# Fewer, wider products in a two-layer decoder: high and low part of x in one matmul, and the first layer's down projection with tokens on partitions

## The chip, the cores and the metric

The kernel runs on one core of a Trainium2 chip. The metric is the device time of one execution in microseconds (us); each kernel is run several times and the median counts. The core has five engines with a queue of instructions each: TensorE (PE in the profile, its weight loads PEld), VectorE (DVE), ScalarE (ACT), GpSimd (POOL) and SyncE (SP), which here issues nearly all DMAs.

## The reference, cut to what matters

Two layers work on 256 tokens of width 1024. In each, a normalized x is projected to queries, keys, values and gates, 24 heads of three kinds of attention follow, and their outputs go through three branch projections, gates and one output projection, which is added to x. Then comes an MLP with a squared ReLU, added to x as well:

```python
merged = gates[:, :, 0] * y_a + gates[:, :, 1] * y_b + gates[:, :, 2] * y_c
x = x + merged @ w_o                                  # output projection
h = rmsnorm(x, norm_mlp)
return x + jnp.square(jax.nn.relu(h @ w_up)) @ w_down # up and down projection
```

w_o is 1024x1024, w_up 1024x4096, w_down 4096x1024, all float32. One normalization follows the second layer.

## The kernel before, in words

All large products run in a rounded float32 form on TensorE, and exactness is kept by splitting: each operand is a high part (rounded) plus a low part (the rest), and a product is three matmuls, low weight by high x, high weight by high x, and high weight by low x. x lies transposed in SBUF, `xres[P, 8, 256]`: 128 channels on partitions, 8 channel tiles (index d or k), 256 tokens.

Weights arrive in 140 pieces of 128x1024 (512 KB) for each layer, in the order in which they are used; `split_one` makes a high part `wh` on ScalarE (L115) and a low part `wl` on VectorE (L116). Four raw buffers and six split buffers turn over. Splits are issued ahead of the work around them (`tc.high_priority`, three pieces ahead).

`proj` (L190 to L197) computes one 128-channel output tile for 256 tokens: for each of 8 k three matmuls of 256 columns, L195 with `lo`, L196 with `hi`, L197 with `hi` and the low part of x. It serves the query, key and gate projections, the branch outputs, the output projection and the up projection. High and low part of x lie in one tile `hl[P, 2, 8, 256]`.

The output projection loops over eight d. Each takes a PSUM bank (`mm_bank` and `t_bank` in turn, two of each), and VectorE adds the bank to `xres` (L511), ScalarE writes the next high part of x times the norm's weight (L155), VectorE its low part (L156), ScalarE squares (L165) and GpSimd adds the squares up (L166). `rms_cols` (L172) turns the sum into one factor for each token, `bcast` (L185) spreads it over partitions; in the first layer its square is `R2`.

The MLP runs over 16 pairs of up tiles. `up_pair` puts both tiles of a pair into the two halves of one bank; ScalarE takes the ReLU from there (L544) and squares (L546), VectorE writes high and low part (L549, L550). The two down products of a pair come one pair later. In the first layer `down` has channels on partitions: for each j and each of 8 d three matmuls of 256 columns (L561 to L563), 768 in all, into `acc2` (two double banks). In the last layer `down_nat` has tokens on partitions: `u` is the stationary operand, 512 weight columns move, in four groups (t, h) of three matmuls for each j (L587 to L589), 384 in all; for its sum x is transposed there (L576) and copied (L577).

At the end of a layer the last TAIL = 4 steps j are done group by group, so that results come out one after another. In the first layer, each d then gets a multiplication by R2 (L648), an addition to xres (L649) and the norm's split; the second layer's values follow (`v_chunk`, L245 to L247: 512 columns, k outermost, so that they can begin with k = 0 before the last d is done). Each engine takes its instructions in the order of a schedule that was laid out when the program was built; within it, ready work of later steps can stand ahead of steps that wait.

Of the kernel before, what the change touches and what calls it, by code (L numbers as in the profile page):

```python
# [41 lines left out]
TAIL = 4  # L42
SKEW = 2
UNIT_RATE = {"v": 2, "qk": 1, "g": 2}
# [14 lines left out]
def trunk(ctx: ExitStack, tc: tile.TileContext, w, x, norms, gfin, consts, out):  # L59
# [18 lines left out]
    def mm_bank():  # L78
        return PS("mm", [P, 512], 2)
# [4 lines left out]
    def t_bank():  # L84
        return PS("t", [P, 512], 2)
# [63 lines left out]
    def hilo_slot():  # L149
        return T("hl", [P, 2, KT, S], 2, F32R)  # L150

    def norm_split(hl, nrm, d):

        g = cst["norms"][:, nrm, d:d + 1]
        act.activation(hl[:, 0, d], xres[:, d], AF.Copy, scale=g)  # L155
        dve.scalar_tensor_tensor(hl[:, 1, d], xres[:, d], g, hl[:, 0, d].bitcast(F32),  # L156
                                 op0=ALU.mult, op1=ALU.subtract)
# [30 lines left out]
    def proj(dst, n, hl, nk=KT, first=True, last=True, koff=0, woff=0):  # L188

        hi, lo = split(n)  # L190
        for k in range(nk):
            c = (woff + k) * P
            a = (first and k == 0)
            z = (last and k == nk - 1)
            pe.matmul(dst, lo[:, c:c + P], hl[:, 0, koff + k], start=a, stop=False, skip_group_check=True)  # L195
            pe.matmul(dst, hi[:, c:c + P], hl[:, 0, koff + k], start=False, stop=False, skip_group_check=True)  # L196
            pe.matmul(dst, hi[:, c:c + P], hl[:, 1, koff + k], start=False, stop=z, skip_group_check=True)  # L197

# [11 lines left out]
    for layer in range(DEPTH):  # L210
# [9 lines left out]
        def normalized():  # L220

            for d in range(KT):
                t = T("sq", [P, S], 3)
                g = cst["norms"][:, 2 * layer, d:d + 1]
                dve.scalar_tensor_tensor(t, xres[:, d], g, R, op0=ALU.mult, op1=ALU.mult)
                act.activation(xh[:, 0, d], t, AF.Copy)
                dve.tensor_tensor(xh[:, 1, d], t, xh[:, 0, d].bitcast(F32), op=ALU.subtract)  # L227

# [3 lines left out]
        def v_chunk(c, n):  # L232
# [5 lines left out]
            for q in range(4):  # L238
                hi, lo = split(n + q)
                for kk in range(2):  # L240
                    k = 2 * q + kk
                    wsl = slice(kk * 512, kk * 512 + 512)
                    for t in range(2):
                        tsl = slice(t * P, t * P + P)
                        pe.matmul(pv[t], xs[:, 0, k, tsl], lo[:, wsl], start=k == 0, stop=False)  # L245
                        pe.matmul(pv[t], xs[:, 0, k, tsl], hi[:, wsl], start=False, stop=False)
                        pe.matmul(pv[t], xs[:, 1, k, tsl], hi[:, wsl], start=False, stop=k == KT - 1)  # L247
            V[c] = T("V", [P, 2, 8, 2, DH], 3, F32R)
# [47 lines left out]
        def o_split(oF, kt):  # L296
            last_exp[0] = act.activation(oT[:, 0, kt], oF, AF.Copy)
            dve.tensor_tensor(oT[:, 1, kt], oF, oT[:, 0, kt].bitcast(F32), op=ALU.subtract)

# [190 lines left out]
        for d in range(KT):  # L490
# [10 lines left out]
            dve.tensor_tensor(m3[:, 0], m3[:, 0], m3[:, 2], op=ALU.add)  # L501
            act.activation(mg[:, 0, d], m3[:, 0], AF.Copy)
            dve.tensor_tensor(mg[:, 1, d], m3[:, 0], mg[:, 0, d].bitcast(F32), op=ALU.subtract)

# [15 lines left out]
        n = base + 76  # L520
        acc2 = [s_bank(), s_bank()]

        def down_dst(d):
            return acc2[d % 2][:, d // 2 % 2, d // 4 * S:(d // 4 + 1) * S]

# [13 lines left out]
        def up_pair(i):  # L539
            p = mm_bank()  # L540
            proj(p[:, 0:S], npc["u", 2 * i], hl)
            proj(p[:, S:2 * S], npc["u", 2 * i + 1], hl)
            s1 = T("wk", [P, 512], WK)
            act.activation(s1, p, AF.Relu)  # L544
            u = T("wk", [P, 512], WK)
            act.activation(u, s1, AF.Square)  # L546
            uh = T("ga", [P, 2, S], KT, F32R)
            ul = T("ga", [P, 2, S], KT, F32R)
            dve.tensor_copy(uh.rearrange("p a b -> p (a b)"), u)  # L549
            dve.tensor_tensor(ul.rearrange("p a b -> p (a b)"), u, uh.rearrange("p a b -> p (a b)").bitcast(F32), op=ALU.subtract)  # L550
            us[i] = (uh, ul)


        def down(j, d):
            hi, lo = split(npc["d", j])
            uh, ul = us[j // 2]
            a = j == 0 and d < 4
            z = j == 2 * npairs - 1
            dst = down_dst(d)
            c = slice(d * P, d * P + P)  # L560
            pe.matmul(dst, lo[:, c], uh[:, j % 2], start=a, stop=False, skip_group_check=True)  # L561
            pe.matmul(dst, hi[:, c], uh[:, j % 2], start=False, stop=False, skip_group_check=True)  # L562
            pe.matmul(dst, hi[:, c], ul[:, j % 2], start=False, stop=z, skip_group_check=True)  # L563

        last = layer == DEPTH - 1
        if last:
# [5 lines left out]
            for t in range(2):  # L572
                for h in range(2):
# [3 lines left out]
                    dve.tensor_copy(xn[t][h], tb)  # L577
            r2 = T("rc", [P, 2], 8)
            dve.tensor_tensor(r2, rcol, rcol, op=ALU.mult)

# [55 lines left out]
        hl = hilo_slot()  # L636
        for d in range(KT):
            if d == 0:
                for e in range(SKEW):
                    for j in range(body, 2 * npairs - 2):  # L640
                        down(j, e)
            if d + SKEW < KT:
# [106 lines left out]
```

## Time and profile before

| | |
|---|---|
| median of 3 runs | 893.87 us (893.34 to 893.88) |
| the profiled execution's own time | 893.46 us |
| its span, first to last instruction | 891.4 us |
| TensorE busy | 878.8 us, 99% |
| VectorE busy | 602.4 us, 68% |
| ScalarE busy | 491.7 us, 55% |
| GpSimd busy | 52.4 us, 6% |
| DMA | 151.47 MB, mean 170 GB/s |
| mean granted TensorE clock | 0.998 of full speed (2.4 GHz) |

A matmul's duration in the profile overlaps the next one's; how fast TensorE goes is read from the distance between two starts, not from the durations. The shares are means over the whole span; the stages differ.

### The profile page before, as it was taken

The page shows a single profiled execution, that of the slowest core. Times are in us where ns is not written, and L with a number is a line of the kernel's source. Part 1 is how long each engine was busy: PE and PEld are TensorE (multiplying, and loading weights), DVE is VectorE, ACT ScalarE, POOL GpSimd, SP SyncE. Part 2 cuts the span into 40 slices and gives each one's busy share as a digit, 9 for nine tenths or more (in the row PEclk, how much of TensorE's full clock was granted, in tenths as well). Part 3 has the DMA queues.
Part 4 walks back from the last instruction along what each step waited for, and adds up shares of the span by engine and source line. Part 5 has one row for each costly group of instructions (what it writes and reads, how often), then busy time and mean ns, then how long its engine had stood idle before and what let it go on. Part 6 is the DMA issues. An engine that isn't in the chain of part 4 may idle for free.

```text
span 891.4 us, 16382 instructions
## 1 busy us (share of the span) xinstructions
PE 878.8 (99%) x6672; PEld 837.8 (94%) x6672; DVE 602.4 (68%) x899; ACT 491.7 (55%) x724; POOL 52.4 (6%) x72
## 2 busy tenths in 40 slices
PE   8999999999999999999999999999999999999996
PEld 6899999999999999999988999999999999999995
DVE  7887787774985455555588878777667865555554
ACT  5655566668465444444466555666573654444442
POOL 6000000000020000000020100000000400000000
PEclk9999999999999999999999999999999999999999
DMA  8764444544656656555556544444555666666641
GB/s 302 232 197 144 140 129 138 158 147 131 199 167 192 193 183 189 182 177 185 165 176 203 167 148 136 141 125 139 164 165 168 194 197 192 186 186 189 187 137 47
DMA packets 43562, 151.47 MB, mean 170 GB/s; under 512 B 4960, under 2 KB 6368, under 8 KB 43488
## 3 DMA queue, kind: packets, MB, share of 16 engines
q1 hardware_dynamic: 43056, 149.90, 54.6%
q8 instruction: 52, 0.85, 0.4%
q10 hardware_dynamic: 432, 0.54, 0.2%
q14 instruction: 22, 0.18, 0.1%
HBM read 149.37 MB, written 1.05 MB: 169 GB/s over the span
## 4 chain that ended last, share of the span: by engine, by line
PE 94%; DVE 3%; issue 1%; DMA 1%; ACT 0%; SPq 0%; POOLq 0%; DVEq 0%; ACTq 0%
PE mm L195 18%; PE mm L197 18%; PE mm L196 18%; PE s L561 3%; PE s L563 3%; PE s L562 3%; PE s L587 3%; PE s L588 3%; PE s L589 3%; PE s L280 2%; PE s L195 2%; PE s L197 2%; PE s L196 2%; PE s L245 2%; DVE wl L116 2%; PE s L247 2%
## 5 line engine op out<-in xcount | busy, mean ns | idle before, releaser
L116 DVE TENSOR_TENSOR wl<-raw,wh 128x1024 fp32r<-128x1024 f32 (+1 forms) x282 | 345.5, 1228 | 228.2 <-ACT wh L115 227.4
L115 ACT ACTIVATE wh<-raw 128x1024 fp32r<-128x1024 f32 (+1 forms) x282 | 295.2, 1051 | 296.4 <-PE mm L197 160.8
L195 PE MATMUL mm<-hl,wl 128*128 128x256 f32 x1344 | 383.2, 285 | 1.4 <-DVE xres L511 1.4
L196 PE MATMUL mm<-hl,wh 128*128 128x256 f32 x1344 | 381.5, 284 | 0.0
L197 PE MATMUL mm<-hl,wh 128*128 128x256 f32 x1344 | 380.1, 284 | 0.0
L195 PEld LDWEIGHTS mm<-hl,wl 128*128 128x128 f32 x1344 | 257.1, 191 | 5.8 <-DVE xres L511 1.8
L196 PEld LDWEIGHTS mm<-hl,wh 128*128 128x128 f32 x1344 | 257.1, 191 | 0.9
L197 PEld LDWEIGHTS mm<-hl,wh 128*128 128x128 f32 x1344 | 256.5, 191 | 0.7 <-DVE hl L227 0.2
L561 PE MATMUL s<-ga,wl 128*128 128x256 f32 x256 | 72.5, 284 | 0.0
L562 PE MATMUL s<-ga,wh 128*128 128x256 f32 x256 | 72.3, 283 | 0.0
L563 PE MATMUL s<-ga,wh 128*128 128x256 f32 x256 | 72.2, 283 | 0.0
L587 PE MATMUL s<-wl,ga 128*128 128x512 f32 x128 | 50.1, 391 | 0.0
L588 PE MATMUL s<-wh,ga 128*128 128x512 f32 x128 | 50.0, 391 | 0.0
L561 PEld LDWEIGHTS s<-ga,wl 128*128 128x128 f32 x256 | 49.1, 192 | 0.5 <-DVE sq L648 0.2
L589 PE MATMUL s<-wh,ga 128*128 128x512 f32 x128 | 49.5, 389 | 0.0
L562 PEld LDWEIGHTS s<-ga,wh 128*128 128x128 f32 x256 | 49.1, 192 | 0.1
L563 PEld LDWEIGHTS s<-ga,wh 128*128 128x128 f32 x256 | 49.0, 192 | 0.2 <-DVE ga L550 0.2
L166 POOL TENSOR_TENSOR acc<-acc,sq 128x256 f32<-128x256 f32 x21 | 20.8, 991 | 404.4 <-ACT sq L165 229.8
L195 PE MATMUL s<-hl,wl 128*128 128x256 f32 x128 | 36.4, 285 | 0.0
L197 PE MATMUL s<-hl,wh 128*128 128x256 f32 x128 | 36.3, 284 | 0.0
L196 PE MATMUL s<-hl,wh 128*128 128x256 f32 x128 | 36.2, 283 | 0.0
L587 PEld LDWEIGHTS s<-wl,ga 128*128 128x128 f32 x128 | 24.1, 188 | 5.0 <-DVE V L622 0.4
(139 smaller groups left out, 1143.4 us busy)
## 6 DMA issues: line engine op xcount, KB each, us to landing
raw<-in_w_dram SPq DMA_DIRECT2D x278, 512.0 KB, 4.0
raw<-in_w_dram SPq DMA_DIRECT2D x4, 256.0 KB, 4.7
xres<-in_x_dram SPq DMA_DIRECT2D x8, 128.0 KB, 5.1
wk<-in_gfin_dram SPq DMA_DIRECT2D x2, 256.0 KB, 4.0
out_dram<-V SPq DMA_DIRECT2D x2, 256.0 KB, 2.3
out_dram<-V ACTq DMA_DIRECT2D x2, 256.0 KB, 2.2
c_maskA<-in_maskA_dram SPq DMA_DIRECT2D x1, 384.0 KB, 5.4
c_rope<-in_rope_dram SPq DMA_DIRECT2D x1, 256.0 KB, 4.9
```

The costliest lines, as they stand in the source:

```text
L115: act.activation(hi[:, c:c + step], r[:, c:c + step], AF.Copy)
L116: dve.tensor_tensor(lo[:, c:c + step], r[:, c:c + step], hi[:, c:c + step].bitcast(F32), op=ALU.subtract)
L166: pool.tensor_tensor(acc, acc, sq, op=ALU.add)
L195: pe.matmul(dst, lo[:, c:c + P], hl[:, 0, koff + k], start=a, stop=False, skip_group_check=True)
L196: pe.matmul(dst, hi[:, c:c + P], hl[:, 0, koff + k], start=False, stop=False, skip_group_check=True)
L197: pe.matmul(dst, hi[:, c:c + P], hl[:, 1, koff + k], start=False, stop=z, skip_group_check=True)
L561: pe.matmul(dst, lo[:, c], uh[:, j % 2], start=a, stop=False, skip_group_check=True)
L562: pe.matmul(dst, hi[:, c], uh[:, j % 2], start=False, stop=False, skip_group_check=True)
L563: pe.matmul(dst, hi[:, c], ul[:, j % 2], start=False, stop=z, skip_group_check=True)
L587: pe.matmul(dst, uh[:, j % 2, k], lo[:, c], start=j == 0, stop=False)
L588: pe.matmul(dst, uh[:, j % 2, k], hi[:, c], start=False, stop=False)
L589: pe.matmul(dst, ul[:, j % 2, k], hi[:, c], start=False, stop=j == 2 * npairs - 1)
```

## The change

The two parts of x move next to each other for each k, `hl[P, 8, 2, 256]`. A new `proj_wide` multiplies the high part of the weight with both at once: for each k one matmul of 256 columns and one of 512, so that the sum with x's high part stands in the left half of a bank and the sum with x's low part in the right half. ScalarE copies the right half to SBUF (`other`, two buffers), and VectorE adds both. The output projection and the up projection use it; the others keep `proj`. An up tile now has a bank of its own; the pair's tiles are added up on VectorE, ReLU and square stay on ScalarE but read SBUF, and the high part of u moves from VectorE to ScalarE.

The first layer's down product uses `down_nat` as the last layer does. Its results (tokens on partitions) are scaled and copied by ScalarE, transposed on TensorE, four 128x128 blocks into one bank, and added to `xres` by VectorE, 128 tokens of four channel tiles at once; the norm's splits come after the second half of the tokens, four d together. `R2` and its broadcast go.

```diff
-        return T("hl", [P, 2, KT, S], 2, F32R)
+        return T("hl", [P, KT, 2, S], 2, F32R)
...
+    def proj_wide(n, hl, bank):
+
+        hi, lo = split(n)
+        for k in range(KT):
+            c = slice(k * P, k * P + P)
+            pe.matmul(bank[:, 0:S], lo[:, c], hl[:, k, 0], start=k == 0, stop=False, skip_group_check=True)
+            pe.matmul(bank, hi[:, c], hl[:, k].rearrange("p a b -> p (a b)"), start=False, stop=k == KT - 1,
+                      skip_group_check=True)
+        other = T("tmp", [P, S], 2)
+        act.activation(other, bank[:, S:2 * S], AF.Copy)
+        return other
...
         for d in range(KT):
             p = mm_bank() if d % 2 else t_bank()
-            proj(p[:, 0:S], base + 68 + d, mg)
+            other = proj_wide(base + 68 + d, mg, p)
             dve.tensor_tensor(xres[:, d], xres[:, d], p[:, 0:S], op=ALU.add)
+            dve.tensor_tensor(xres[:, d], xres[:, d], other, op=ALU.add)
             norm_split(hl, 2 * layer + 1, d)
             sumsq(d, acc)
         rcol = rms_cols(acc)
-        if layer < DEPTH - 1:
-            R2 = T("tmp", [P, S], 2)
-            act.activation(R2, bcast(rcol), AF.Square)
...
         def up_pair(i):
-            p = mm_bank()
-            proj(p[:, 0:S], npc["u", 2 * i], hl)
-            proj(p[:, S:2 * S], npc["u", 2 * i + 1], hl)
-            s1 = T("wk", [P, 512], WK)
-            act.activation(s1, p, AF.Relu)
-            u = T("wk", [P, 512], WK)
-            act.activation(u, s1, AF.Square)
+            t = T("wk", [P, 2, S], WK)
+            for a in range(2):
+                p = mm_bank()
+                other = proj_wide(npc["u", 2 * i + a], hl, p)
+                dve.tensor_tensor(t[:, a], p[:, 0:S], other, op=ALU.add)
+            act.activation(t, t, AF.Relu)
+            u = T("wk", [P, 2, S], WK)
+            act.activation(u, t, AF.Square)
             uh = T("ga", [P, 2, S], KT, F32R)
             ul = T("ga", [P, 2, S], KT, F32R)
-            dve.tensor_copy(uh.rearrange("p a b -> p (a b)"), u)
-            dve.tensor_tensor(ul.rearrange("p a b -> p (a b)"), u, uh.rearrange("p a b -> p (a b)").bitcast(F32), op=ALU.subtract)
+            act.activation(uh, u, AF.Copy)
+            dve.tensor_tensor(ul, u, uh.bitcast(F32), op=ALU.subtract)
             us[i] = (uh, ul)
...
-        groups = [(t, h) for t in range(2) for h in range(2)] if last else [(d,) for d in range(KT)]
-        one = down_nat if last else down
+        groups = [(t, h) for t in range(2) for h in range(2)] if last else [(t, h) for h in range(2) for t in range(2)]
+        one = down_nat
...
+        for i, (t, h) in enumerate(groups):
+            if i == 0:
                 for j in range(body, 2 * npairs - 2):
-                    down(j, d + SKEW)
+                    one(j, t, h)
+            if i + 1 < len(groups):
+                for j in range(body, 2 * npairs - 2):
+                    one(j, *groups[i + 1])
             for j in range(2 * npairs - 2, 2 * npairs):
-                down(j, d)
-            tmp = T("sq", [P, S], 3)
-            dve.tensor_tensor(tmp, down_dst(d), R2, op=ALU.mult)
-            dve.tensor_tensor(xres[:, d], xres[:, d], tmp, op=ALU.add)
-            norm_split(hl, 2 * layer + 2, d)
-            sumsq(d, acc)
+                one(j, t, h)
+            y = T("wk", [P, 512], WK)
+            act.activation(y, acc2[h][:, t], AF.Copy, scale=r2[:, t:t + 1])
+            tb = t_bank()
+            for d in range(4):
+                pe.transpose(tb[:, d * P:(d + 1) * P], y[:, d * P:(d + 1) * P], ident)
+            x4 = xres[:, 4 * h:4 * h + 4, t * P:(t + 1) * P]
+            dve.tensor_tensor(x4, x4, tb.rearrange("p (a b) -> p a b", a=4), op=ALU.add)
+            if t == 1:
+                for d in range(4 * h, 4 * h + 4):
+                    norm_split(hl, 2 * layer + 2, d)
+                    sumsq(d, acc)
```

## Rows read from the trace of the kernel before

**Rows 1.** The page: busy time (share of the span) and instructions of each engine.

```profile
PE 878.8 (99%) x6672; PEld 837.8 (94%) x6672; DVE 602.4 (68%) x899; ACT 491.7 (55%) x724; POOL 52.4 (6%) x72
```

**Rows 2.** Stretches: us, busy PE, PEld, DVE, ACT, POOL, clock, DMA share, GB/s.

```profile
250.00:268.50 18.50, 17.50 (x142) 16.92 (x141) 18.07 (x24) 13.69 (x24) 6.54 (x7) 1.00 0.57 192
438.50:466.50 28.00, 27.96 (x163) 24.51 (x162) 23.64 (x36) 16.36 (x28) 5.87 (x7) 1.00 0.51 163
339.72:409.00 69.28, 69.28 (x580) 69.28 (x579) 35.69 (x36) 32.28 (x37) 0.00 (x0) 1.00 0.59 183
```

**Rows 3.** Timeline of PE in the first MLP: first and last of 27 matmuls (start, us).

```profile
339.72 0.28 PE L195 MATMUL mm<-hl,wl 128*128 128x256 f32 x1
...
342.84 0.28 PE L197 MATMUL mm<-hl,wh 128*128 128x256 f32 x1
```

**Rows 4.** Chain in order of time, second MLP: one instruction, ten pairs apart.

```profile
739.11 0.23 PE s L588
...
851.30 0.23 PE s L588
```

**Rows 5.** Timeline of PE in the second MLP: four transposes among matmuls.

```profile
711.13 0.60 PE L576 MATMUL t<-c_ident,xres 128*128 128x128 f32 x4
711.49 0.36 PE L197 MATMUL mm<-hl,wh 128*128 128x256 f32 x1
711.69 0.28 PE L195 MATMUL mm<-hl,wl 128*128 128x256 f32 x1
```

**Rows 6.** Timeline of PE's weight loads around the broadcast for R2.

```profile
273.31 0.19 PEld L195 LDWEIGHTS mm<-hl,wl 128*128 128x128 f32 x1
273.43 0.31 PEld L185 LDWEIGHTS t<-sq,ones 128*128 128x128 f32 x2
...
273.98 0.19 PEld L197 LDWEIGHTS mm<-hl,wh 128*128 128x128 f32 x1
```

**Rows 7.** Timeline of DVE, output projection's end in the first layer.

```profile
250.21 0.42 DVE L511 TENSOR_TENSOR xres<-xres,t 128x256 f32<-128x256 f32 x1 [3.70 <-PE t L197]
250.55 0.41 DVE L511 TENSOR_TENSOR xres<-xres,mm 128x256 f32<-128x256 f32 x1
...
265.47 0.41 DVE L511 TENSOR_TENSOR xres<-xres,mm 128x256 f32<-128x256 f32 x1
...
267.33 0.95 DVE L156 SCALAR_TENSOR_TENSOR hl<-xres,c_norms,hl 128x256 fp32r<-128x256 f32 x1
```

**Rows 8.** Timeline of PE there: what waited, and the last step of k.

```profile
265.93 0.39 PE L195 MATMUL mm<-hl,wl 128*128 128x256 f32 x1 [0.84 <-DVE xres L511]
...
268.42 0.40 PE L197 MATMUL mm<-hl,wh 128*128 128x256 f32 x2
```

**Rows 9.** One line's instructions: count, durations in ns min/median/max (L166 of that stretch alone).

```profile
L156 DVE SCALAR_TENSOR_TENSOR hl<-xres,c_norms,hl x32: 472/831/968, 5.0 to 706.5; 128x256 fp32r<-128x256 f32 x32
L649 DVE TENSOR_TENSOR xres<-xres,sq x8: 410/418/987, 442.5 to 463.2; 128x256 f32<-128x256 f32 x8
L166 POOL TENSOR_TENSOR acc<-acc,sq x7: 747/805/1441, 255.7 to 266.9; 128x256 f32<-128x256 f32 x7
```

**Rows 10.** Groups of instructions by line and shape: busy us, mean ns.

```profile
L116 DVE TENSOR_TENSOR wl<-raw,wh 128x1024 fp32r<-128x1024 f32 x278 | 341.5, 1231 | 222.5 <-ACT wh L115 221.7
L115 ACT ACTIVATE wh<-raw 128x1024 fp32r<-128x1024 f32 x278 | 292.7, 1057 | 292.1 <-PE mm L197 160.8 <-PE s L563 38.9 <-PE s L589 33.7
L155 ACT ACTIVATE hl<-xres,c_norms 128x256 fp32r<-128x256 f32 x32 | 15.8, 497 | 7.8 <-DVE xres L649 4.6 <-DVE xres L511 3.1
L165 ACT ACTIVATE sq<-xres 128x256 f32<-128x256 f32 x21 | 8.4, 402 | 0.0
L544 ACT ACTIVATE wk<-mm 128x512 f32<-128x512 f32 x32 | 18.6, 581 | 4.7 <-PE mm L197 4.7
L546 ACT ACTIVATE wk<-wk 128x512 f32<-128x512 f32 x32 | 20.3, 633 | 1.0
L550 DVE TENSOR_TENSOR ga<-wk,ga 128x512 fp32r<-128x512 f32 x32 | 22.2, 692 | 1.1
```

More of the change, by code (lines that the diff above doesn't have):

```diff
@@ L42 @@
 TAIL = 4
-SKEW = 2
 UNIT_RATE = {"v": 2, "qk": 1, "g": 2}
@@ L149, in hilo_slot @@
     def hilo_slot():
-        return T("hl", [P, 2, KT, S], 2, F32R)
+        return T("hl", [P, KT, 2, S], 2, F32R)
     def norm_split(hl, nrm, d):
         g = cst["norms"][:, nrm, d:d + 1]
-        act.activation(hl[:, 0, d], xres[:, d], AF.Copy, scale=g)
-        dve.scalar_tensor_tensor(hl[:, 1, d], xres[:, d], g, hl[:, 0, d].bitcast(F32),
+        act.activation(hl[:, d, 0], xres[:, d], AF.Copy, scale=g)
+        dve.scalar_tensor_tensor(hl[:, d, 1], xres[:, d], g, hl[:, d, 0].bitcast(F32),
                                  op0=ALU.mult, op1=ALU.subtract)
@@ L194, in proj @@
             z = (last and k == nk - 1)
-            pe.matmul(dst, lo[:, c:c + P], hl[:, 0, koff + k], start=a, stop=False, skip_group_check=True)
-            pe.matmul(dst, hi[:, c:c + P], hl[:, 0, koff + k], start=False, stop=False, skip_group_check=True)
-            pe.matmul(dst, hi[:, c:c + P], hl[:, 1, koff + k], start=False, stop=z, skip_group_check=True)
+            pe.matmul(dst, lo[:, c:c + P], hl[:, koff + k, 0], start=a, stop=False, skip_group_check=True)
+            pe.matmul(dst, hi[:, c:c + P], hl[:, koff + k, 0], start=False, stop=False, skip_group_check=True)
+            pe.matmul(dst, hi[:, c:c + P], hl[:, koff + k, 1], start=False, stop=z, skip_group_check=True)
+    def proj_wide(n, hl, bank):
[8 more added lines that the diff above has]
+        return other
     acc = T("acc", [P, S], 1)
@@ L225, in normalized @@
                 dve.scalar_tensor_tensor(t, xres[:, d], g, R, op0=ALU.mult, op1=ALU.mult)
-                act.activation(xh[:, 0, d], t, AF.Copy)
-                dve.tensor_tensor(xh[:, 1, d], t, xh[:, 0, d].bitcast(F32), op=ALU.subtract)
+                act.activation(xh[:, d, 0], t, AF.Copy)
+                dve.tensor_tensor(xh[:, d, 1], t, xh[:, d, 0].bitcast(F32), op=ALU.subtract)
         V = {}
@@ L244, in v_chunk @@
                         tsl = slice(t * P, t * P + P)
-                        pe.matmul(pv[t], xs[:, 0, k, tsl], lo[:, wsl], start=k == 0, stop=False)
-                        pe.matmul(pv[t], xs[:, 0, k, tsl], hi[:, wsl], start=False, stop=False)
-                        pe.matmul(pv[t], xs[:, 1, k, tsl], hi[:, wsl], start=False, stop=k == KT - 1)
+                        pe.matmul(pv[t], xs[:, k, 0, tsl], lo[:, wsl], start=k == 0, stop=False)
+                        pe.matmul(pv[t], xs[:, k, 0, tsl], hi[:, wsl], start=False, stop=False)
+                        pe.matmul(pv[t], xs[:, k, 1, tsl], hi[:, wsl], start=False, stop=k == KT - 1)
             V[c] = T("V", [P, 2, 8, 2, DH], 3, F32R)
@@ L296, in o_split @@
         def o_split(oF, kt):
-            last_exp[0] = act.activation(oT[:, 0, kt], oF, AF.Copy)
-            dve.tensor_tensor(oT[:, 1, kt], oF, oT[:, 0, kt].bitcast(F32), op=ALU.subtract)
+            last_exp[0] = act.activation(oT[:, kt, 0], oF, AF.Copy)
+            dve.tensor_tensor(oT[:, kt, 1], oF, oT[:, kt, 0].bitcast(F32), op=ALU.subtract)
         def pv_mm(po, head, kt, ph, pl, first, last):
@@ L501, in trunk @@
             dve.tensor_tensor(m3[:, 0], m3[:, 0], m3[:, 2], op=ALU.add)
[L502 to L503 removed]
+            act.activation(mg[:, d, 0], m3[:, 0], AF.Copy)
+            dve.tensor_tensor(mg[:, d, 1], m3[:, 0], mg[:, d, 0].bitcast(F32), op=ALU.subtract)
         acc = T("acc", [P, S], 1)
@@ L539, in up_pair @@
         def up_pair(i):
-            p = mm_bank()
-            proj(p[:, 0:S], npc["u", 2 * i], hl)
-            proj(p[:, S:2 * S], npc["u", 2 * i + 1], hl)
-            s1 = T("wk", [P, 512], WK)
-            act.activation(s1, p, AF.Relu)
-            u = T("wk", [P, 512], WK)
-            act.activation(u, s1, AF.Square)
+            t = T("wk", [P, 2, S], WK)
[6 more added lines that the diff above has]
+            act.activation(u, t, AF.Square)
             uh = T("ga", [P, 2, S], KT, F32R)
             ul = T("ga", [P, 2, S], KT, F32R)
-            dve.tensor_copy(uh.rearrange("p a b -> p (a b)"), u)
-            dve.tensor_tensor(ul.rearrange("p a b -> p (a b)"), u, uh.rearrange("p a b -> p (a b)").bitcast(F32), op=ALU.subtract)
+            act.activation(uh, u, AF.Copy)
+            dve.tensor_tensor(ul, u, uh.bitcast(F32), op=ALU.subtract)
             us[i] = (uh, ul)
[L554 to L563, printed above, removed]
         last = layer == DEPTH - 1
@@ L577, in trunk @@
                     dve.tensor_copy(xn[t][h], tb)
-            r2 = T("rc", [P, 2], 8)
-            dve.tensor_tensor(r2, rcol, rcol, op=ALU.mult)
+        r2 = T("rc", [P, 2], 8)
+        dve.tensor_tensor(r2, rcol, rcol, op=ALU.mult)
         def down_nat(j, t, h):
```

8 lines of the change are left out of this document (removed).

## Prediction

> **What bounds the kernel now.** I read the busy shares first, then a table of stretches, then the distances between starts on TensorE, and last VectorE's timeline where TensorE waits at all. TensorE is busy 878.8 of 891.4 us [rows 1], and inside the first MLP 69.28 of 69.28 us, while VectorE and ScalarE work about half of it (35.69 and 32.28) [rows 2]. So the number of matmuls and what each occupies set the time nearly everywhere, and a cheaper matmul stream is worth its full amount wherever the other engines keep up. The exception is the end of the output projection: from 250.0 to 268.5 VectorE is busy 18.07 of 18.50 us [rows 2], and the second layer's stretch looks the same. There TensorE waits, 0.84 us in one place, for an addition on VectorE [rows 8].
>
> **What a matmul occupies.** In a stream of 256 columns, 26 starts lie 3.12 us apart: 0.1200 us each [rows 3]. For 512 columns I take the second MLP: ten pairs take 112.19 us, 11.22 a pair [rows 4]. A pair there has 48 matmuls of 256 columns (5.76 us) and 24 of 512, so these take 5.46 us, 0.2275 each. Twice 256 is 0.240, so one instruction fewer for the same columns is worth 0.0125 us. This is the whole source of the gain; no column is saved.
>
> By the Trainium skill (TensorE: Matmul & The Clock Gate, "Back-to-back issue gap") an isolated stream has N/2.4 + 2.5 ns between starts, 109 and 216 ns here, and joining two would save only 2.5 ns: over 1,024 instructions 2.6 us instead of 12.8, and the sum below would end slower, near 899.7. The rows show 120 and 227.5 ns, so I go by them.
>
> **Terms on TensorE.**
> - Output projection 8 d x 8 k x 2 layers = 128 steps, up projection 32 x 8 x 2 = 512 steps. A step was 0.360 us and becomes 0.1200 + 0.2275 = 0.3475: 640 x 0.0125 = -8.0 us.
> - First layer's down: 768 x 0.1200 = 92.16 us become 384 x 0.2275 = 87.36: -4.8.
> - 16 transposes are added. From the first of four (711.13) to the second matmul behind them (711.69) it is 0.56 us; without them 0.12 would lie between the two matmuls: 0.44 [rows 5]. Four such groups: +1.76.
> - R2's broadcast goes: its two matmuls stretch 0.67 us where 0.24 would stand [rows 6]: -0.43. Its small VectorE and ScalarE work is off the path.
>
> If nothing waited: -11.5.
>
> **End of the output projection.** VectorE runs without a pause from 250.21 to 268.28 (267.33 + 0.95) [rows 7]: eight additions, eight weight splits, eight low parts. The change puts eight second additions into that queue, and behind each of them stand the next split and low part, for which TensorE waits. From one such addition's start to the next it is 0.34 us [rows 7], so the lower price is 8 x 0.34 = 2.7. Upper price: an addition with both inputs in SBUF has a median of 0.418 but once took 0.987 [rows 9]; eight of those are 7.9. The low parts show what lengthens them: 0.47 alone, up to 0.97 [rows 9], and seven GpSimd additions of 0.8 us (median) stand in this stretch [rows 9]. These are as many after the change, so I take little on top: 3.0.
>
> The Trainium skill (SBUF — State Buffer, "Who interferes with whom") says that a VectorE instruction with two SBUF inputs is held by a GpSimd instruction that reads SBUF, and one with a PSUM input is not. The trace's 0.987 fits it. By the rule it is only the second of the two additions that can be held; were all eight held, the layer's 3.0 would be 7.9.
>
> What TensorE sees: today the last k's matmuls (268.42) come just as their low part does (268.28) [rows 7, 8]. After the change TensorE would be there 0.6 us earlier by its shorter steps (46 x 0.0125), and VectorE starts some 0.4 earlier (32 steps before 250.2), so the wait grows by 3.0 + 0.6 - 0.4 = 3.2 us. Next in line is a bank: the third up tile needs the first one's bank, which today is released by a ReLU with a whole pair's work as cover. Now it has only the last step of the second tile (0.35). From the last matmul's start: 0.39 to its end, a ScalarE copy of about 0.40 (nearest row L165, 0.402 [rows 10]), an addition of 0.41, three hand-overs of 0.05: 1.35, less 0.35 and the usual 0.23: 0.8. Together 4.0 in the first layer. In the second, the 16 transposes that exist there already (1.76) can fill some 1.4 of it: 2.6. Sum +6.6. Bounds: 0 (the schedule puts the additions behind splits that nobody waits for yet, and other ready matmuls ahead) to 2 x (7.9 + 0.2 + 0.8) = 17.8. I stay in the lower half because VectorE's additions are counted at a measured row and GpSimd's work doesn't grow.
>
> **In the MLP's loop** a bank is needed again only after the pair's other tile (2.78) and two downs (5.46), 8.2 us; copy and addition take 0.9 and at worst stand behind one split each (1.06 and 1.23 [rows 10]): hidden with 5 us to spare. ScalarE gets two copies (0.8) and the high part (0.63) for each pair of 11 us, VectorE two additions for a cast of 0.43: both stay under two thirds busy [rows 2, 10]. u is ready later: from the last up matmul 0.40 + 0.41 + three ScalarE passes of about 0.63 [rows 10] + 0.69, with two splits between about 5.5 us, against 11 us of cover in the loop, 5.56 for the first pair: +0.2 a layer, +0.4 (bounds 0 and 2). At each loop's end that cover is 5.5 us of matmuls for j = 28 and 29.
>
> **Layer boundary.** Before, each of eight d came out by itself, and the stretch is nearly all TensorE (27.96 of 28.00 us) [rows 2]. Now four channel tiles wait for the last group: copy 0.58, transposes 0.44, addition 0.69, then 0.50 and 0.48 for the first high and low part [rows 5, 9, 10] and five hand-overs: 3.2 us to k = 4, each further k at most 0.90 by ScalarE's two instructions [rows 10]. Cover is the value projection on k = 0 to 3, 24 matmuls x 0.2275 = 5.46, and then 1.37 a k. So it is hidden if the weight splits come through: +0.5. Bounds: 0, and without the cover 3.2 + 3 x 0.9 = 5.9.
>
> **Sum.** -12.8 + 1.76 - 0.43 + 6.6 + 0.4 + 0.5 = -4.0. Against the profiled execution's own 893.46 that is **889.5 us**; the median of the runs is 0.4 higher, within their spread. About 0.2%, 1.8 us, can be told from no change: faster means under 892.1, slower above 895.7.
>
> **Rivals.**
> - *Full gain.* The additions fit into the queue, or TensorE finds other work: -11.5, 882.0. For it: half of VectorE and ScalarE is free in the MLP. Against it: 18.07 of 18.50 us at the one place where it counts [rows 2]. With partial cover up to 885. Chance 0.22.
> - *The layer boundary opens.* The last four channel tiles come after the cover, because splits and norm work queue on ScalarE: 5.4 more, 894.9. VectorE is 84% busy there already (23.64 of 28.00) [rows 2]. Chance 0.08.
> - *VectorE's queue at the output projection* (the other sign): every second addition is held by a GpSimd one, 0.99 each: 17.8 instead of 6.6, 900.7. Slower begins at 12.8 for both layers, 6.4 each instead of 3.3. For it: low parts there take 0.83 in the median [rows 9]. Against: GpSimd has only seven additions in a layer and already meets other work. Chance 0.10.
> - *The wide step doesn't pay.* The pause of some 13 ns belongs to columns or to two operands that lie apart, and 512 interleaved columns take 0.240: 8.0 less gain, 897.5. Against it: 512 contiguous columns at 0.2275 [rows 4]. Chance 0.04. The Trainium skill's rule on the gap (TensorE: Matmul & The Clock Gate, "Back-to-back issue gap") would end near here as well.
> - My forecast, 886 to 892.5: 0.50. The rest, 0.06, is spread around no change.
>
> **Numbers.** Faster: 0.22 + most of 0.50 + a little of the rest, 0.76. Slower: 0.10 + 0.04 less what stays small, 0.12. Same: 0.12. The range is 882 to 895.5: from full gain to beyond an open boundary, leaving out the long queue and the unpaid step and a little below.
>
> **What would show it.** Right: starts of 256 and 512 columns alternating at 0.12 and 0.2275 in the up projection, pairs of 11.0 us in the first MLP instead of 11.52 and 11.0 instead of 11.22 in the second, and a gap on TensorE of several us after the last output projection that waits for VectorE, followed by one for a bank. Wrong: no new gap there (then 882 to 885), a gap at the value projection's fifth k, a pair longer than 11.1 us, or additions of xres near 1 us.

## The result and the profile after

The changed kernel takes 901.76 us (median of 4 runs, 900.62 to 903.74), the kernel before beside it 893.88 us: a ratio of 1.0094, interval 1.0082 to 1.0106. By the medians it is slower by 7.9 us, where 889.5 and a range up to 895.5 had been forecast. The profiled execution took 900.62, 7.2 us more than the profiled one of before.

The page, busy times after [rows 1]:

```profile
span 898.9 us, 14578 instructions
...
PE 873.8 (97%) x5662; PEld 785.3 (87%) x5662; DVE 614.8 (68%) x934; ACT 535.1 (60%) x839; POOL 52.0 (6%) x72
```

TensorE has 5.0 us less to do in a span that is 7.5 longer: it waits. The table of waits of TensorE after says for what (engine, tile, line, releaser; us in total, times, longest):

```profile
PE mm L203 <- DVE xres L522: 4.8, 4, 2.0
PE t L203 <- DVE xres L522: 4.2, 2, 2.1
PE mm L203 <- DVE rc L574: 2.3, 1, 2.3
PE mm L204 <- DVE hl L155: 1.2, 2, 0.6
...
PE mm L203 <- DVE wk L550: 0.8, 1, 0.8
PE t L645 <- ACT wk L642: 0.8, 1, 0.8
```

The first five rows shown all stand between the output projection's fifth tile and the third up tile, 13.3 us for both layers. Before, the same table has 1.7 us there; the largest is the 0.84 of [rows 8]. TensorE's timeline in the first layer shows each of them (start, length, in brackets the wait and its releaser; 254.67 begins the sixth output tile, 260.21 the eighth):

```profile
249.29 0.40 PE L204 MATMUL mm<-hl,wh 128*128 128x512 f32 x1
251.78 0.39 PE L203 MATMUL t<-hl,wl 128*128 128x256 f32 x1 [2.09 <-DVE xres L522]
...
254.67 0.28 PE L203 MATMUL mm<-hl,wl 128*128 128x256 f32 x1
...
260.21 0.28 PE L203 MATMUL mm<-hl,wl 128*128 128x256 f32 x1
...
265.17 0.36 PE L203 MATMUL mm<-hl,wl 128*128 128x256 f32 x1 [2.03 <-DVE xres L522]
...
267.49 0.50 PE L204 MATMUL mm<-hl,wh 128*128 128x512 f32 x1 [0.57 <-DVE hl L155]
...
269.43 0.38 PE L203 MATMUL mm<-hl,wl 128*128 128x256 f32 x1 [0.71 <-DVE xres L522]
...
275.78 0.36 PE L203 MATMUL mm<-hl,wl 128*128 128x256 f32 x1 [2.25 <-DVE rc L574]
```

The first wait comes after four output tiles, when all four banks are full and the fifth tile needs one back. At 265.17 the eighth output tile's eight steps are done and the first up tile begins: it needs the sixth output tile's bank (2.03; 1.33 in the second layer), and the second up tile at 269.43 the eighth one's (0.71). In between, the first up tile waits for the low part of the fifth channel tile (0.57). The last wait is the third up tile's, which needs the first one's bank. Its row names L574, the VectorE instruction that ended last before it, but no matmul of that tile reads `rc`; the addition L550 right ahead of L574 releases the bank, and the second layer's row for the same place names it. What a bank waits for stands in the queues of ScalarE and VectorE after the change. ScalarE's timeline:

```profile
249.08 1.06 ACT L114 ACTIVATE wh<-raw 128x1024 fp32r<-128x1024 f32 x1 [3.20 <-PE t L204]
250.04 0.36 ACT L207 ACTIVATE tmp<-t 128x256 f32<-128x256 f32 x1
...
272.99 1.06 ACT L114 ACTIVATE wh<-raw 128x1024 fp32r<-128x1024 f32 x1 [2.30 <-PE mm L204]
273.95 0.37 ACT L207 ACTIVATE tmp<-mm 128x256 f32<-128x256 f32 x1
```

and VectorE's, which had begun the additions without a pause in [rows 7]:

```profile
250.17 1.23 DVE L115 TENSOR_TENSOR wl<-raw,wh 128x1024 fp32r<-128x1024 f32 x1 [3.83 <-ACT wh L114]
251.31 0.41 DVE L522 TENSOR_TENSOR xres<-xres,t 128x256 f32<-128x256 f32 x1
...
274.08 1.23 DVE L115 TENSOR_TENSOR wl<-raw,wh 128x1024 fp32r<-128x1024 f32 x1 [0.35 <-ACT wh L114]
275.22 0.42 DVE L550 TENSOR_TENSOR wk<-mm,tmp 128x256 f32<-128x256 f32 x1
```

At both places the engine is idle until TensorE ends something, and then takes a weight split first: the matmuls that end a tile also free a split buffer, so the split for a piece needed only later and the copy that would release the bank become ready nearly together, and the split stands ahead in the order. ScalarE loses 1.06 us to it. VectorE loses about as much again, since the low part of that same piece waits for its high part and stands ahead of the addition. The addition starts at 251.31, and TensorE goes on at 251.78; the copy, over at 250.40, is not what it waits for there.

In the second layer the same wait has a second consequence. TensorE's timeline there, and the granted clock (last number but two) in stretches of 2 us:

```profile
690.79 0.40 PE L204 MATMUL mm<-hl,wh 128*128 128x512 f32 x1
693.27 0.39 PE L203 MATMUL t<-hl,wl 128*128 128x256 f32 x1 [2.09 <-DVE xres L522]
...
694.79 0.41 PE L203 MATMUL t<-hl,wl 128*128 128x256 f32 x1
...
695.43 0.41 PE L203 MATMUL t<-hl,wl 128*128 128x256 f32 x1
...
697.73 0.28 PE L203 MATMUL mm<-hl,wl 128*128 128x256 f32 x1
```

```profile
692.00:694.00 2.00, 0.73 (x4) 0.69 (x5) 2.00 (x3) 2.00 (x4) 0.00 (x0) 0.99 0.14 18
694.00:696.00 2.00, 2.00 (x8) 1.67 (x7) 2.00 (x4) 1.96 (x5) 0.00 (x0) 0.50 0.74 252
```

After 2.48 us without a start the clock falls to 0.50, its level of 1.2 GHz: a step takes 0.64 us (694.79 to 695.43), and the tile of eight steps 4.46 (693.27 to 697.73). The fifth tile of the first layer took 2.89 after the same wait (251.78 to 254.67), at a clock of 1.00: the fall costs 1.6 us, and not each wait brings one. Of the four runs, two with a mean clock of 0.996 took 900.6 and 900.8, two with 0.992 took 902.8 and 903.7.

What the change was to bring is there, but smaller. The MLP's loops after, by the first step of two tiles that follow each other and the pair's first down product (first MLP), and by one instruction a pair apart (second MLP):

```profile
331.42 0.28 PE L203 MATMUL mm<-hl,wl 128*128 128x256 f32 x1
...
337.06 0.40 PE L582 MATMUL s<-wl,ga 128*128 128x512 f32 x1
...
342.52 0.28 PE L203 MATMUL mm<-hl,wl 128*128 128x256 f32 x1
...
747.04 0.40 PE L582 MATMUL s<-wl,ga 128*128 128x512 f32 x1
...
758.14 0.40 PE L582 MATMUL s<-wl,ga 128*128 128x512 f32 x1
```

Sixteen steps take 5.64 us, 0.3525 each, where 0.3475 had been worked out. In the output projection it is less: the sixteen steps from 254.67 to 260.21 lie 0.346 apart, as forecast. In the loops a pair takes 11.10 in both layers, where 11.0 had been expected; before it was 11.52 in the first (96 x 0.1200) and 11.22 in the second [rows 4]. The down products' 24 matmuls take 5.46 (337.06 to 342.52), 0.2275 each, as forecast.

### The profile page after: what moved, and what is told of

Read it like the earlier page. It is cut to its first block, busy times and chain, and to the rows that moved or that the text cites. A ratio compares the mean times of both kernels' runs of the same rounds, so it can differ in the third digit from the quotient of the medians.

```text
span 898.9 us, 14578 instructions
## 1 busy us (share of the span) xinstructions
PE 873.8 (97%) x5662; PEld 785.3 (87%) x5662; DVE 614.8 (68%) x934; ACT 535.1 (60%) x839; POOL 52.0 (6%) x72
## 4 chain that ended last, share of the span: by engine, by line
PE 92%; DVE 4%; DMA 1%; issue 1%; ACT 1%; SPq 0%; POOLq 0%; DVEq 0%; ACTq 0%
PE mm L204 14%; PE mm L194 11%; PE mm L196 10%; PE mm L195 10%; PE mm L203 7%; PE s L582 6%; PE s L584 6%; PE s L583 6%; PE s L291 2%; PE s L194 2%; PE s L196 2%; PE s L195 2%; PE s L256 2%; PE s L258 2%; PE s L257 2%; DVE wl L115 2%
## 5 line engine op out<-in xcount | busy, mean ns | idle before, releaser
L195 PE MATMUL mm<-hl,wh 128*128 128x256 f32 x768 | 218.6, 285 | 0.0
L196 PE MATMUL mm<-hl,wh 128*128 128x256 f32 x768 | 217.7, 285 | 0.0
L204 PE MATMUL mm<-hl,wh 128*128 128x512 f32 x576 | 206.2, 398 | 1.4 <-DVE hl L155 1.2
L195 PEld LDWEIGHTS mm<-hl,wh 128*128 128x128 f32 x768 | 146.7, 191 | 0.3
L196 PEld LDWEIGHTS mm<-hl,wh 128*128 128x128 f32 x768 | 146.4, 191 | 0.2
L204 PEld LDWEIGHTS mm<-hl,wh 128*128 128x128 f32 x576 | 108.0, 188 | 27.2 <-DVE hl L155 2.6
L582 PE MATMUL s<-wl,ga 128*128 128x512 f32 x256 | 100.4, 392 | 0.2 <-ACT ga L556 0.2
L583 PE MATMUL s<-wh,ga 128*128 128x512 f32 x256 | 99.7, 390 | 0.0
L584 PE MATMUL s<-wh,ga 128*128 128x512 f32 x256 | 99.4, 390 | 0.0
L584 PEld LDWEIGHTS s<-wh,ga 128*128 128x128 f32 x256 | 48.1, 188 | 10.4
L583 PEld LDWEIGHTS s<-wh,ga 128*128 128x128 f32 x256 | 48.1, 188 | 10.2
L582 PEld LDWEIGHTS s<-wl,ga 128*128 128x128 f32 x256 | 48.1, 188 | 9.7 <-ACT ga L556 0.6
L557 DVE TENSOR_TENSOR ga<-wk,ga 128x512 fp32r<-128x512 f32 x32 | 22.1, 691 | 22.9 <-ACT ga L556 22.9
L196 PE MATMUL s<-hl,wh 128*128 128x256 f32 x128 | 36.3, 284 | 0.0
```

Of the source, the lines that this page charges most:

```text
L195: pe.matmul(dst, hi[:, c:c + P], hl[:, koff + k, 0], start=False, stop=False, skip_group_check=True)
L196: pe.matmul(dst, hi[:, c:c + P], hl[:, koff + k, 1], start=False, stop=z, skip_group_check=True)
L204: pe.matmul(bank, hi[:, c], hl[:, k].rearrange("p a b -> p (a b)"), start=False, stop=k == KT - 1, skip_group_check=True)
L557: dve.tensor_tensor(ul, u, uh.bitcast(F32), op=ALU.subtract)
L582: pe.matmul(dst, uh[:, j % 2, k], lo[:, c], start=j == 0, stop=False)
L583: pe.matmul(dst, uh[:, j % 2, k], hi[:, c], start=False, stop=False)
```

## Experiments

Two theories stood against each other: the loss is at the output projection, where copies and additions come too late (A), or in the MLP, where VectorE's and ScalarE's new work delays u or the layer boundary. The first four kernels ran on one chip beside 893.51 for before, the next four beside 893.68, the last three beside 893.74.

**Output projection narrow again.** The rest as changed.

```diff
-            other = proj_wide(base + 68 + d, mg, p)
+            proj(p[:, 0:S], base + 68 + d, mg)
             dve.tensor_tensor(xres[:, d], xres[:, d], p[:, 0:S], op=ALU.add)
-            dve.tensor_tensor(xres[:, d], xres[:, d], other, op=ALU.add)
```

> The changed kernel with the output projection back at three matmuls of 256 columns a step and one addition; up and down projection stay as changed. Theory A (the loss sits at the end of the output projection: second additions and bank releases in VectorE's and ScalarE's queues): the waits of 2.3, 2.2, 0.7 and 1.0 us there go, what is left is the bank wait at the third up tile; 889 to 892 us. Rival B (the loss is the up projection's, a bank for each tile and a longer way to u): about 899 to 901. Rival C (the loss is the first layer's down projection with its transposes): about 899 to 901.

Measured 894.99 us (11 runs, 892.62 to 895.49), ratio 1.0010 (1.0001 to 1.0019). Of 7.9 us of loss 1.5 are left, so most of it goes with the wide output projection, but the time is 3 to 6 us above the one expected. A row of the waits and a stretch behind the third up tile's, in this kernel:

```profile
PE mm L203 <- DVE wk L549: 3.9, 2, 2.5
```

```profile
274.00:276.00 2.00, 2.00 (x8) 1.71 (x7) 0.36 (x1) 1.54 (x3) 0.00 (x0) 0.50 0.77 221
```

The third up tile's bank stays late, and the clock falls behind it. The one run whose mean clock was 0.999 took 892.62; those at 0.994 took 894.9 to 895.5.

**Only the output projection wide.** Up and down projection as before.

```diff
-                p = mm_bank()
-                other = proj_wide(npc["u", 2 * i + a], hl, p)
...
+            proj(p[:, 0:S], npc["u", 2 * i], hl)
+            proj(p[:, S:2 * S], npc["u", 2 * i + 1], hl)
...
-        one = down_nat
+        one = down_nat if last else down
```

> Only the output projection is wide; up and down projection as in the kernel before. Theory A: slower than before by what the first kernel of this call gains, 902 to 907 us, with the same waits on TensorE after the first four tiles and before the second up tile. Rivals B and C: 892 to 894, since the wide steps save 1 to 1.6 us.

Measured 902.73 (4 runs), ratio 1.0101 (1.0087 to 1.0115). This part alone loses 9.2 us: theory A holds for it, and neither the up nor the down projection's new form is needed for that loss. The fifth output tile's waits are the changed kernel's, and the clock is at 0.50 here too (254 to 256 us). A row of its waits:

```profile
PE t L204 <- DVE xres L523: 4.2, 2, 2.1
```

**Only the first layer's down changed.** Output and up projection narrow.

```diff
-            other = proj_wide(base + 68 + d, mg, p)
+            proj(p[:, 0:S], base + 68 + d, mg)
...
-                other = proj_wide(npc["u", 2 * i + a], hl, p)
...
+            proj(p[:, 0:S], npc["u", 2 * i], hl)
+            proj(p[:, S:2 * S], npc["u", 2 * i + 1], hl)
```

> Only the first layer's down projection is changed (tokens on partitions); output and up projection as before. Theory A: 384 matmuls of 0.2275 us for 768 of 0.12, 4.8 us less, 16 transposes and small waits at the layer's end cost 1.8 to 2.8, the broadcast saves 0.4: 890 to 892 us. Rival C: slower than before, 896 or more.

Measured 890.33 (5 runs), ratio 0.9961 (0.9949 to 0.9974): 3.2 us faster. The forecast's own terms for this part (down, transposes, R2, boundary) add up to -3.0. The first experiment is this kernel with the wide up projection added, and it is 4.7 us slower (894.99). So rival B is true in part: the up projection loses as well, at the third up tile's bank, where the forecast had it gain.

**Banks released first.** All parts as changed; only the order in which ScalarE and VectorE take their instructions differs.

```diff
+EPRI = 600
...
-        act.activation(other, bank[:, S:2 * S], AF.Copy)
+        with tc.high_priority(offset=EPRI):
+            act.activation(other, bank[:, S:2 * S], AF.Copy)
...
-            dve.tensor_tensor(xres[:, d], xres[:, d], p[:, 0:S], op=ALU.add)
+            with tc.high_priority(offset=EPRI):
+                dve.tensor_tensor(xres[:, d], xres[:, d], p[:, 0:S], op=ALU.add)
...
-                dve.tensor_tensor(t[:, a], p[:, 0:S], other, op=ALU.add)
+                with tc.high_priority(offset=EPRI):
+                    dve.tensor_tensor(t[:, a], p[:, 0:S], other, op=ALU.add)
```

> The changed kernel with one difference in order: the copy and the addition that release a bank of a wide projection stand ahead of weight splits in ScalarE's and VectorE's queues, the work is the same. Theory A1 (the banks come late because splits of 1.06 and 1.23 us stand in front of copy and addition): the waits after the first four tiles fall from 2.3 to about 1 us in both layers, the one at the third up tile from 2.3 to about 1, and TensorE's clock does not fall to its lower level at the second layer's output projection: 893 to 897 us. Rival A2 (VectorE has too much work there in whatever order): the waits move behind later weights, 899 us or more.

Measured 890.67 (5 runs, 890.50 to 891.24), ratio 0.9966 (0.9954 to 0.9979). It is 2.8 us faster than the kernel before, where the change is 7.9 slower: with the same instructions, their order alone is worth 10.7 us, more than either theory expected. ScalarE, TensorE and TensorE's waits in this kernel:

```profile
249.25 0.38 ACT L209 ACTIVATE tmp<-t 128x256 f32<-128x256 f32 x1 [3.15 <-PE t L205]
249.53 1.05 ACT L115 ACTIVATE wh<-raw 128x1024 fp32r<-128x1024 f32 x1
```

```profile
250.14 0.39 PE L204 MATMUL t<-hl,wl 128*128 128x256 f32 x1 [0.23 <-DVE xres L525]
...
271.19 0.39 PE L204 MATMUL mm<-hl,wl 128*128 128x256 f32 x1 [0.36 <-DVE wk L554]
```

```profile
PE mm L205 <- DVE hl L156: 2.8, 2, 1.4
PE mm L204 <- DVE xres L525: 1.6, 2, 0.8
PE t L204 <- DVE xres L525: 1.1, 4, 0.3
...
PE mm L204 <- DVE wk L554: 0.4, 1, 0.4
```

The copy now stands before the split, the fifth output tile waits 0.23 instead of 2.09 and the third up tile 0.36 instead of 2.25. The splits that come later delay TensorE no more than before (waits for weight splits are 2.3 us in all, in the changed kernel 2.5): 13.3 us of waits have become 5.9. Of these, 2.8 are for low parts of x, the wait that the forecast had named. Copy and addition were always moved together, so no run tells which of the two counts more.

**The two halves of that order.** Releases first at the output projection alone, and at the up projection alone: the edit above without its third part, and without its second (with the copy's priority for that caller only).

```diff
-    def proj_wide(n, hl, bank):
+    def proj_wide(n, hl, bank, first=False):
...
+        if first:
+            with tc.high_priority(offset=EPRI):
+                act.activation(other, bank[:, S:2 * S], AF.Copy)
```

> The changed kernel; only the output projection's copies and additions stand ahead of weight splits, the up projection's stay behind them. Theory A1: the waits of 2.2 us after the first four tiles go in both layers and with them the fall of the clock in the second; the wait at the third up tile (2.3 us) stays and may now bring the clock down there: 893 to 897 us. Rival A2 (too much work on VectorE in whatever order): 899 or more.

Measured 895.69 (10 runs, 893.89 to 897.63), ratio 1.0020 (1.0011 to 1.0029), as expected. The fifth tile's wait is gone and the third up tile's remains:

```profile
PE mm L204 <- DVE rc L580: 2.3, 1, 2.3
...
PE t L204 <- DVE xres L528: 1.0, 4, 0.3
```

> The changed kernel; only the up projection's copies and additions stand ahead of weight splits, the output projection's stay behind them. Theory A1: the wait at the third up tile falls from 2.3 to about 0.5 us (first layer) and from 0.8 to none (second), the waits of 2.2 us after the first four tiles stay, with a fall of the clock behind at least one of them: 897.5 to 900 us. Rival A2: 900.5 or more.

Measured 898.16 (5 runs), ratio 1.0049 (1.0036 to 1.0062), as expected, and the waits are the other way about:

```profile
PE t L204 <- DVE xres L527: 4.2, 2, 2.1
...
PE mm L204 <- DVE wk L556: 0.4, 1, 0.4
```

Beside the kernel before these are 2.0 and 4.5 slower, so from the change's 7.9 the output projection's order takes 5.9 us, the up projection's 3.4, both together 10.7.

**GpSimd without additions in the MLP's norm.** The kernel as changed, but only the first channel tile's squares enter that norm: the other tiles' part of its sum is left out.

```diff
-            pool.tensor_tensor(acc, acc, sq, op=ALU.add)
+            if add:
+                pool.tensor_tensor(acc, acc, sq, op=ALU.add)
...
-            sumsq(d, acc)
+            sumsq(d, acc, False)
```

> The changed kernel without GpSimd's additions of the squares in the MLP's norm: only the first channel tile's squares count, so that part of the norm's sum is left out. Theory P (second additions are held by GpSimd's: 0.95 us instead of 0.42 for about half of them, and that lies on the way to the second up tile's bank and to the last low part): every second addition takes 0.41 to 0.5, the wait before the second up tile falls from 2.0 to about 0 to 1 us, 897 to 900 us. Rival A1 alone (order, not GpSimd): additions shorter, but waits and time stay within 1 us, 900.5 to 902.5.

Measured 901.54 (6 runs, 898.24 to 903.4), ratio 1.0081 (1.0064 to 1.0099). By the median nothing is gained. The second additions (count, ns min/median/max), first in the changed kernel, then in this one:

```profile
L523 DVE TENSOR_TENSOR xres<-xres,tmp x16: 410/686/962, 253.1 to 711.8; 128x256 f32<-128x256 f32 x16
```

```profile
L524 DVE TENSOR_TENSOR xres<-xres,tmp x16: 410/416/425, 253.5 to 710.5; 128x256 f32<-128x256 f32 x16
```

Without GpSimd's work all take 0.41 us; with it the median is 0.69 and the longest 0.96, as the 0.987 of [rows 9] had hinted. The Trainium skill (SBUF — State Buffer, "Who interferes with whom") says that a VectorE instruction with both inputs in SBUF contends with a GpSimd instruction that reads SBUF; these rows agree with it. The waits show why little comes of it:

```profile
PE mm L204 <- DVE wk L551: 5.0, 2, 2.5
...
PE mm L204 <- DVE rc L174: 0.9, 2, 0.5
...
PE mm L204 <- DVE xres L523: 0.3, 1, 0.3
```

The wait of 2.0 us, which the expectation puts before the second up tile, is the first one's: it falls from 2.03 to 0.45 in the first layer (the row that names L174), the second one's from 0.71 to 0.25, but the third one's now is 2.5 us in both layers. Runs with a mean clock of 0.996 took 898.2 and 898.3 here, 2.4 us less than the changed kernel's at 0.996; the others stand at 0.992 and lower and took 901.5 to 903.4. So the hold is real and worth about 2 us between runs of equal clock (two of each kernel), and it is the smaller part of the change's loss.

**Narrow output projection, up's releases first.** The first experiment and the up half of the order together.

```diff
-            other = proj_wide(base + 68 + d, mg, p)
+            proj(p[:, 0:S], base + 68 + d, mg)
...
+                with tc.high_priority(offset=EPRI):
+                    dve.tensor_tensor(t[:, a], p[:, 0:S], other, op=ALU.add)
```

> Up and down projection as changed, the output projection with three matmuls of 256 columns as before, and copy and addition that release an up tile's bank ahead of weight splits. Theory A1 (order of the releases decides; the wide up projection then keeps its 0.12 us a pair, 3.8 us in all): 890.3 of the kernel with only the down projection changed, less 3.8, plus a bank wait of about 0.8 in each layer: 887 to 889 us, no fall of the clock after the first layer's output projection. Rival D (an up tile in a bank of its own costs more than its matmuls save, in whatever order): 890.5 or more.

Measured 888.73 (5 runs, 888.25 to 888.83), ratio 0.9943 (0.9931 to 0.9955): the lowest ratio of all, 5.0 us below the kernel before. Against the version with the wide output projection in the same order (0.9966) it gains 2 us more: there the wide form loses even when its banks are released at once.

**Four banks instead of an order.** The first experiment, with up tiles that take `t_bank` and `mm_bank` in turn.

```diff
-                p = mm_bank()
+                p = mm_bank() if a else t_bank()
```

> As the first experiment (narrow output projection, releases behind splits), but the two tiles of an up pair take a bank of mm and one of t in turn, four banks in all, so that four tiles can run before a bank must be free. Theory A1: the wait of 2.5 us at the third up tile goes in both layers and no fall of the clock follows: 888 to 891 us instead of 895. Rival (the wait is for u or for hl, not for a bank): 894 to 895.

Measured 889.35 (5 runs), ratio 0.9952 (0.9940 to 0.9965). With four banks the splits may stand first. TensorE's only wait between 262 and 276 us is the one that the kernel before has as well [rows 8]:

```profile
265.94 0.39 PE L203 MATMUL mm<-hl,wl 128*128 128x256 f32 x1 [0.85 <-DVE xres L522]
```

**Both.** Four banks and up's releases first, on the narrow output projection.

```diff
-                p = mm_bank()
+                p = mm_bank() if a else t_bank()
...
+                with tc.high_priority(offset=EPRI):
+                    dve.tensor_tensor(t[:, a], p[:, 0:S], other, op=ALU.add)
```

> Releases ahead of splits and four banks for the up projection, narrow output projection. Theory A1: one of the two measures already takes nearly all of the wait at the third up tile; together 887 to 889 us. If banks still held TensorE up elsewhere in the MLP's loop: 886 or less.

Measured 889.59 (5 runs), ratio 0.9955 (0.9942 to 0.9969): nothing more. Either cure takes the third up tile's wait in the first layer (0.7 us is left with the order, none with four banks); with four banks one of 1.1 stands in the second layer, where the transposes use `t` as well. The intervals of the three versions overlap.

**The 512 columns first.** The fastest version, with the two matmuls of a step exchanged, to see whether their order sets the pace.

```diff
-            pe.matmul(bank[:, 0:S], lo[:, c], hl[:, k, 0], start=k == 0, stop=False, skip_group_check=True)
-            pe.matmul(bank, hi[:, c], hl[:, k].rearrange("p a b -> p (a b)"), start=False, stop=k == KT - 1,
+            pe.matmul(bank, hi[:, c], hl[:, k].rearrange("p a b -> p (a b)"), start=k == 0, stop=False,
...
+            pe.matmul(bank[:, 0:S], lo[:, c], hl[:, k, 0], start=False, stop=k == KT - 1, skip_group_check=True)
```

> As the kernel with the narrow output projection and releases ahead of splits, but in each wide step the matmul of 512 columns stands before the one of 256. Asked is why a wide step in the MLP's loop takes 0.3525 us and not the 0.3475 that the two distances add up to. If it is the change of width from one matmul to the next, order doesn't matter: 888 to 889.5 us and pairs of 11.10. If it is the 256 columns' short time before a weight load for 512, the other order may change the pace to 0.346, pairs of 11.0: 885 to 886.5.

Measured 894.07 (11 runs, 892.36 to 895.48), ratio 1.0002 (0.9993 to 1.0011). The pace stays at 0.352 to 0.353 us a step, so the order of the widths is not its cause. That 5 us are lost has another reason: of the 4.0 between the two profiled executions, 3.0 are waits for up tiles' banks (3.7 us against 0.7). The timelines of ScalarE and TensorE show the longest:

```profile
269.42 1.06 ACT L115 ACTIVATE wh<-raw 128x1024 fp32r<-128x1024 f32 x1 [3.02 <-PE mm L204]
270.39 0.37 ACT L209 ACTIVATE tmp<-mm 128x256 f32<-128x256 f32 x1
```

```profile
272.13 0.50 PE L204 MATMUL mm<-hl,wh 128*128 128x512 f32 x1 [2.28 <-DVE wk L552]
```

The split stands in front again in spite of the copy's priority. The likely reason, read from the edit and not tested: the high part of the weight is last used one matmul earlier, so its buffer, and with it the next split, is ready before the copy. This edit, made for another purpose, repeats the loss.

## Why the prediction was wrong

**The step that failed is "End of the output projection".** It forecast +6.6 us for both layers. The account of the profiled execution: the measured step lengths give -5.2 for the wide steps (128 x 0.011 in the output projection, whose steps lie 0.346 to 0.350 apart, 512 x 0.0075 in the up projection), and the forecast's other sure terms (-4.8, +1.76, -0.43, +0.5) are kept; that makes -8.2. Measured is +7.2. So 15.4 us were lost where 7.0 (with the 0.4 for u) were forecast. The waits account for 11.6 of it (13.3 less 1.7) and one fall of the clock for 1.6; the other 2 us are not itemised. What failed first is the premise that VectorE starts its additions "some 0.4 earlier" than 250.21: the first one starts at 251.31, behind a split. By the step's own terms:

- *The queue of second additions* (+3.2 in the first layer): the waits there are 2.03 + 0.57 + 0.71 = 3.3 us, before 0.84, so +2.5. Near in size, but not the wait that was named: only 0.57 is for a low part, 2.74 for the banks of the first and second up tile, which the output tiles' additions release late. GpSimd's hold on half of the additions, which the upper bound had for all, is in it.
- *The third up tile's bank* (+0.8): 2.25. The text took copy and addition to start at once, with three hand-overs of 0.05. It had itself counted one split each, 1.06 and 1.23, "at worst" ahead of them in the MLP's loop, and left them out at the one place without cover. Releasing first brings the wait to 0.36.
- *The fifth output tile's bank*: no term at all. What releases a wide tile's bank stands behind splits, and four banks are full after four tiles: 2.09 us in each layer, before 0.2 at most. It is the largest single miss, 4 us.
- *The clock*: no term. The forecast kept 1.00 throughout, as before has it. Behind the wait of 2.09 us the next tile ran at 0.50 in the second layer and at 1.00 in the first; the fall took 1.6 us.

That the order is the cause is shown by the kernel with the releases first: the same instructions, 10.7 us less. Its loss by the same account is -2.8 + 8.2 = 5.4 us, near the forecast's 7.0. The forecast's sum fits that kernel (890.67 against 889.5) rather than the one that was built, and partly by luck: the loss was set 1.6 too high and the gain of the wide steps 2.8 too high.

**The price of a wide step** was too good in the MLP's loops. 0.1200 and 0.2275 were read from streams of one width [rows 3, 4]; alternating they take 0.3525 together in the loop, and -8.0 becomes -5.2. In parts of the output projection the forecast's 0.3475 is reached (0.346), so the two widths alone do not set the pace. By the formula of the Trainium skill (TensorE: Matmul & The Clock Gate, "Back-to-back issue gap") joining two would save an estimated 2.5 ns. The rows show 7.5 in the loop and up to 14 in the output projection, more than this rule in both places. Why the two stretches differ is open; the exchange of the two widths left the loop's pace as it was.

**The rivals.** *VectorE's queue at the output projection* (900.7, chance 0.10) names the right place, sign and nearly the time, but for the most part by a wrong mechanism: half of the second additions are held, and without GpSimd's additions the median is still 901.5 (2.4 us less at equal clock). The queue's order did more than what is held in it. The 0.83 that spoke for this rival covers all 32 low parts [rows 9]; the eight of that stretch have a median of 0.960. *Full gain* falls with the waits. *The layer boundary opens* does not happen: the only wait there is the transposes' on the scaled copy, 0.78 us, against 0.5 forecast, and none at the value projection's fifth k. *The wide step doesn't pay* is a third true (2.8 of 8.0). Of the forecast's own signs of being wrong, additions near 1 us came (0.96), and the pair of 11.10 lies at its limit.

**Right were** the first layer's down product (-3.2 measured alone, -3.0 forecast), the boundary, the banks in the MLP's loop, whose 5 us to spare hold (no wait for a bank there), and u (one wait for it, 0.2 us). The boundary's 3.2 us takes hand-overs of 0.1, where 0.05 stands elsewhere; the sum does not use it.

## What to carry to other kernels

A bank's release runs through the in-order queues of the engines that empty it: where fewer banks than tiles in flight are free, put into the sum what stands ahead of the emptying instruction, prefetch work above all, and look whether one event makes both ready. Moving that work behind the release, or doubling the banks, was worth more here than the cheaper matmuls. Read a pace from a stream of the mix that will run, and allow for what the clock may take on top of a wait on TensorE.

## What the runs showed of the hardware

- TensorE's clock fell to 0.50 of full speed behind a gap of 2.48 us between two starts in the second layer, and stayed at 1.00 behind a gap of 2.49 in the first layer of the same execution. Eight steps then took 4.46 us instead of 2.89. Runs of the same kernel with a mean clock of 0.996 took 900.6 and 900.8, those with 0.992 took 902.8 and 903.7, so most of the spread goes with the clock.
- Matmuls of 256 and 512 columns in turn took 0.352 to 0.353 us for both in the MLP's loop, in either order, and 0.346 in parts of the output projection; streams of one width add up to 0.3475.
- VectorE's additions with both inputs in SBUF took 0.41 us without GpSimd beside them, and up to 0.96 with it.
